# Splitting a projection's weights one stage earlier, and one product for two halves, in a two-block attention kernel

## The chip, the cores and the metric

The kernel runs on one core of one Trainium2 chip, in one launch. The metric is device time in microseconds. The kernel before takes 3167.22 us, the median of 3 runs from 3156.71 to 3170.61.

## The reference

A sequence of 2048 tokens of 1024 channels goes through two blocks, all in fp32.

```python
def first_block(x, ...):
    h = rms_norm(x, g_pre) * (1.0 + scale) + shift
    qa, ka, va, fa, za, qb, kb, vb, zb = split(h @ w_in)
    oa = forgetting_attention(qa, ka, va, fa + b_fgate) * silu(za)      # 8 heads of 64
    qb, kb = rope(qb), rope(kb)                                         # 8 query heads, 2 key heads
    ob = sliding_window_sink_attention(qb, kb, vb, sinks) * silu(zb)    # window of 128
    y = concatenate([oa, ob]) @ w_out
    return x + gate * rms_norm(y, g_post)

def second_block(x, ...):
    h = concatenate([meta_tokens, x])                                   # 16 + 2048 rows
    q_a, c_kv, q_idx, k_idx, w_idx, gate_a, q_h, f_h, i_h, gate_h = split(h @ w_in_2)
    a = dsa_attention(q_a, rms_norm_2(c_kv), q_idx, k_idx, w_idx, rel_bias, w_uk, w_uv) * silu(gate_a)
    r = rms_norm_2(hgrn2(q_h, f_h, i_h)) * silu(gate_h)
    y = concatenate([a, r]) @ w_out_2                                   # 1024 x 1024
    return layer_norm(DN_ALPHA * h + y)[16:]

def rope(x, positions):       # per head: the first 32 channels and the last 32
    x1, x2 = x[..., :half], x[..., half:]
    return concatenate([x1 * cos - x2 * sin, x2 * cos + x1 * sin])
```

`dsa_attention` lets every query see the meta rows and its 256 best keys by an index score; `hgrn2` is a gated recurrence over chunks of 64.

## The kernel before

Values and weights of fp32 are split into a high and a low fp16 part, and a product is three fp16 products (high by high, high by low, low by high) summed in PSUM. A 128-column product over 1024 channels for 512 tokens is so 24 matmuls (`mm3_T`, L319). The Tile scheduler fixes the order of each engine's instructions ahead of time from the program order and its priorities; on the chip every engine and every DMA queue works its list in that order. Nearly all DMAs of the parts below are issued by SyncE.

**The stages**, by the profile: a prologue; the first projection (`blocks1`), woven from about 200 us on with the forgetting attention, to about 950 us; the rest of that attention, the sliding attention and the first output projection, to about 1500; the second projection (`phase_proj2`) with the index scores and the top-k selection, to about 2215; and the third stage (`phase_dsa`), in which 32 steps of the sparse attention (4 groups of queries by 8 heads) are woven with the recurrence's chunks and the second output projection with its norm.

**Weights of a projection** come in blocks through `stream` (L298), which loads one block ahead. `load_w` (L249) loads a block in four pieces of 256 KB into a ring of 4 buffers with tag "wraw" (L260), squares each on ScalarE (L262) and sums the squares over the partitions with a small matmul `wsum` (L239 in `sum_scale`), for which the result bank has the tag "st" and rotates with products of that tag. From the sum come a scale and, per piece, a product by it on VectorE (L282), a cast to the high part `whi` on ScalarE (L283) and the low part `wlo` on GpSimd (L284). The second projection has twelve blocks: forget gate, gates, queries of the attention, queries of the recurrence and the input gate, two each (`fh fh gh gh ga ga qh qh qa qa ih ih`). Each product of a block of queries leaves PSUM by `evac_T` (L361: `ehi` on ScalarE L345, low part on VectorE L346, store L366). VectorE also runs the selection's scans (L1788) in this stage.

**The second output projection's weights** are used in the third stage. After the fourth block `wo_scale` (L1097) loads them once, through the same ring, for their scale alone. `phase_dsa` calls `load_wo` in its first step, with priority −3000, and that loads them again, in 8 pieces of 512 KB, into a single buffer, and splits them:

```python
    for k in range(KK):
        raw = rp.tile([128, D], F32, name="raw", tag="z" if tag == "pp" else "xr", bufs=2 if tag == "pp" else 1)
        nc.sync.dma_start(raw, src[k * 128:(k + 1) * 128])                             # L1116
        for c in (slice(0, 512), slice(512, D)):
            nc.scalar.activation(hi[:, k, c], raw[:, c], AF.Copy, scale=K.ows)         # L1118
            nc.vector.scalar_tensor_tensor(lo[:, k, c], raw[:, c], K.ows, hi[:, k, c], ...)  # L1119
```

**The sliding attention's keys and queries** are rotated as they leave PSUM, in `rotated` (L504). Its weights are laid out with the first halves of the heads' channels ahead of the second halves: 2 key heads give m = 64 columns of each half, the queries m = 128. For each of 4 groups of 512 tokens it makes two products, one for each half, in two banks of tag "pp", and combines them with the tables of cosines and sines: two products by a table on VectorE (L523, L524) and an addition or subtraction on GpSimd (L525), in tiles `ra` of a ring of 4, stored by `store_rot` (L477).

## Time and profile before

| | before |
|---|---|
| median of 3 runs | 3167.22 us |
| the profiled execution | 3170.48 us |
| its span | 3168.7 us |
| its granted TensorE clock, mean | 0.938 |
| TensorE busy | 2822.7 us, 89% |
| VectorE, ScalarE, GpSimd busy | 66%, 53%, 46% |

The profile records one execution. Its span runs from the first to the last instruction, and the execution's own time lies 1.8 us above it. Times in the rows are counted from the start of the span. Matmuls are pipelined: one that is recorded as 0.38 us long may have its successor start 0.22 us after it.

### The profile page before, as it was taken

How to read it: one execution, taken by the hardware profiler on the slowest of the kernel's cores; microseconds unless marked ns; L12 is line 12 of the kernel's file. 1: busy time of each engine (PE TensorE's matmuls, PEld its weight loads, DVE VectorE, ACT ScalarE, POOL GpSimd, SP SyncE). 2: the span in 40 equal slices, each digit the busy share in tenths (PEclk: the TensorE clock that was granted, in tenths of full speed). 3: DMA queues.
4: the chain of work that ended last, by engine and by line, in shares of the span. 5: the costliest groups of instructions: out<-in, count | busy, mean ns of one | idle time of the engine just before them, and what ended most of it. 6: DMA issues, size and time to landing. Idle time of an engine off the chain costs nothing. (4 is left out here: it accounts for less than half of the span.)

```text
span 3168.7 us, 65862 instructions
## 1 busy us (share of the span) xinstructions
PE 2822.7 (89%) x25152; PEld 1858.8 (59%) x25152; DVE 2101.6 (66%) x5073; ACT 1686.9 (53%) x3058; POOL 1450.2 (46%) x1241
## 2 busy tenths in 40 slices
PE   7899999999997899999998889899678888988997
PEld 5554444477884555544445665358566566666663
DVE  7523765566678676646499699830578778888763
ACT  4423665576566655634356466321455456657763
POOL 3211446564333555534233433610456567768752
PEclk9899999999996799999999989899679989999998
DMA  6222343532235343334433532222753444443331
GB/s 235 82 87 84 105 129 111 173 95 69 79 94 167 109 142 108 124 91 157 111 97 101 160 125 73 89 91 63 182 159 102 137 133 113 118 117 110 122 97 59
DMA packets 271184, 364.28 MB, mean 115 GB/s; under 512 B 60205, under 2 KB 192033, under 8 KB 269705
## 3 DMA queue, kind: packets, MB, share of 16 engines
q1 hardware_dynamic: 270424, 359.96, 37.8%
q8 instruction: 199, 3.26, 0.4%
q14 instruction: 129, 1.05, 0.1%
q10 hardware_dynamic: 432, 0.02, 0.0%
HBM read 247.05 MB, written 112.82 MB: 114 GB/s over the span
## 5 line engine op out<-in xcount | busy, mean ns | idle before, releaser
L752 POOL TENSOR_TENSOR plo<-p,phi 128x512 f16<-128x512 f32 (+3 forms) x600 | 664.9, 1121 | 569.9 <-ACT phi L748 360.0
L748 ACT CAST phi<-p 128x512 f16<-128x512 f32 (+3 forms) x649 | 347.0, 554 | 84.2 <-PE po L778 75.1
L746 ACT ACTIVATE p<-pst,shift,dci 128x512 f32<-128x512 f32 (+4 forms) x352 | 247.4, 716 | 137.2 <-POOL plo L752 46.7
L778 PE MATMUL po<-v,plo 128*128 128x65 f16 x2176 | 270.1, 196 | 35.0 <-POOL plo L752 27.9
L776 PE MATMUL po<-v,phi 128*128 128x65 f16 x2176 | 286.4, 197 | 5.3 <-ACT phi L748 4.2
L777 PE MATMUL po<-v,phi 128*128 128x64 f16 x2176 | 285.3, 198 | 0.0
L778 PEld LDWEIGHTS <-plo 128*128 128x128 f16 x2424 | 234.7, 101 | 79.2 <-POOL plo L752 46.8
L746 ACT ACTIVATE p<-pst,shift,fci 128x512 f32<-128x512 f32 (+1 forms) x320 | 220.1, 710 | 113.1 <-PE pst L984 70.2
L963 DVE TENSOR_REDUCE mu<-p 128x1 f32<-128x512 f32 (+2 forms) x320 | 188.4, 603 | 130.1 <-PE p L959 83.3
L776 PEld LDWEIGHTS <-phi 128*128 128x128 f16 x2424 | 236.1, 100 | 48.8 <-ACT phi L748 11.4
L284 POOL TENSOR_TENSOR wlo<-wraw,whi 128x512 f16<-128x512 f32 (+3 forms) x116 | 149.9, 1310 | 216.9 <-ACT whi L283 214.0
L2058 DVE CUSTOM_DVE_ANT_0 jk<-p,mk 128x512 bf16<-128x512 f32 (+2 forms) x320 | 193.4, 604 | 80.5 <-PE p L2052 32.8
L777 PEld LDWEIGHTS <-phi 128*128 128x128 f16 x2424 | 235.6, 100 | 15.3 <-issue 1.8
L337 PE MATMUL pp<-whi,hhi 128*128 128x256 f16 (+2 forms) x824 | 235.0, 286 | 7.7 <-ACT whi L283 5.7
L339 PE MATMUL pp<-whi,hlo 128*128 128x256 f16 (+2 forms) x824 | 233.2, 285 | 4.2 <-POOL hlo L465 4.2
L338 PE MATMUL pp<-wlo,hhi 128*128 128x256 f16 (+2 forms) x824 | 234.7, 285 | 0.6 <-POOL wlo L284 0.6
L326 PE MATMUL pp<-hhi,whi 128*128 128x512 f16 (+2 forms) x496 | 190.7, 384 | 4.4 <-DVE ra L523 4.4
L328 PE MATMUL pp<-hhi,wlo 128*128 128x512 f16 (+2 forms) x496 | 190.3, 384 | 0.0
L327 PE MATMUL pp<-hlo,whi 128*128 128x512 f16 (+2 forms) x496 | 190.0, 383 | 0.0
L328 PEld LDWEIGHTS <-wlo 128*128 128x128 f16 (+2 forms) x1000 | 99.7, 100 | 122.6 <-POOL wlo L284 10.9
L326 PEld LDWEIGHTS <-whi 128*128 128x128 f16 (+2 forms) x1000 | 100.5, 101 | 120.1 <-issue 10.2
L327 PEld LDWEIGHTS <-whi 128*128 128x128 f16 (+2 forms) x1000 | 99.9, 101 | 117.3 <-issue 16.0
(666 smaller groups left out, 8933.6 us busy)
## 6 DMA issues: line engine op xcount, KB each, us to landing
wraw<-in_w_in_dram SPq DMA_DIRECT2D x88, 256.0 KB
d_z<-er SPq DMA_DIRECT2D x128, 128.0 KB
bT<-d_rb SPq DMA_DIRECT2D x32, 384.0 KB
wa<-in_w_ada_dram SPq DMA_DIRECT2D x8, 1024.0 KB
x<-in_x_dram SPq DMA_DIRECT2D x16, 512.0 KB
d_k<-ehi SPq DMA_DIRECT2D x32, 256.0 KB
d_q<-ehi SPq DMA_DIRECT2D x32, 256.0 KB
QA<-d_q SPq DMA_DIRECT2D x64, 128.0 KB
```

What stands on the lines that cost most here:

```text
L326: nc.tensor.matmul(ps, lhsT=whi, rhs=hhi[:, kk, :], start=kk == 0, stop=False)
L327: nc.tensor.matmul(ps, lhsT=whi, rhs=hlo[:, kk, :], start=False, stop=False)
L328: nc.tensor.matmul(ps, lhsT=wlo, rhs=hhi[:, kk, :], start=False, stop=kk == KK - 1)
L337: nc.tensor.matmul(ps, lhsT=hhi[:, kk, s], rhs=whi, start=kk == 0, stop=False)
L338: nc.tensor.matmul(ps, lhsT=hhi[:, kk, s], rhs=wlo, start=False, stop=False)
L339: nc.tensor.matmul(ps, lhsT=hlo[:, kk, s], rhs=whi, start=False, stop=kk == KK - 1)
L746: nc.scalar.activation(p, s, AF.Exp, scale=ci[:m], bias=K.shift[:m])
L748: nc.scalar.copy(hi, p)
L752: e.tensor_tensor(lo, p, hi, op=ALU.subtract)
L776: nc.tensor.matmul(o, lhsT=hi, rhs=v[:, :65], start=first, stop=False, **kw)
L777: nc.tensor.matmul(o[:, 1:65], lhsT=hi, rhs=v[:, 65:129], start=False, stop=False, **kw)
L778: nc.tensor.matmul(o, lhsT=lo, rhs=v[:, :65], start=False, stop=last, **kw)
```

## The change

For the rotated keys (m = 64) one product with all 128 columns takes the place of two with 64. Its first 64 rows are the one operand, and ScalarE copies its last 64 rows to a fifth tile of the `ra` ring, whose first row is partition 0, for the other. The queries are made as before.

The split of the second output projection's weights moves into the second projection. `wo_parts` stands in the list of blocks between the two blocks of queries `qa`: 16 rounds, each loading 256 KB into the "wraw" ring, casting, subtracting and storing both parts to DRAM (`d_wo`) from a tile of the same ring. The third stage reads the parts with four DMAs of 1 MB (`read_wo`), with the priority that `load_wo` had.

```diff
             for g in range(NG):
-                p = [ps.tile([128, 512], F32, name="pp")[:m] for _ in range(2)]
-                for a in range(2):
-                    mm3_T(K, p[a], w, a * m, h[g])
+                if m == 64:
+                    pb = ps.tile([128, 512], F32, name="pp")
+                    mm3_T(K, pb, w, 0, h[g])
+                    z = sp.tile([128, 512], F32, name="ra", tag="ra", bufs=4)[:m]
+                    nc.scalar.copy(z, pb[m:])
+                    p = [pb[:m], z]
+                else:
+                    p = [ps.tile([128, 512], F32, name="pp")[:m] for _ in range(2)]
+                    for a in range(2):
+                        mm3_T(K, p[a], w, a * m, h[g])
...
+def wo_parts(K, pool, src):
+    nc = K.nc
+    for k in range(KK):
+        for c in range(2):
+            raw = pool.tile([128, 2, 256], F32, name="wraw", tag="wraw", bufs=K.rbufs).rearrange("p a n -> p (a n)")
+            nc.sync.dma_start(raw, src[k * 128:(k + 1) * 128, c * 512:c * 512 + 512])
+            x = pool.tile([128, 2, 512], F16, name="wparts", tag="wraw", bufs=K.rbufs)
+            nc.scalar.activation(x[:, 0], raw, AF.Copy, scale=K.ows)
+            nc.vector.scalar_tensor_tensor(x[:, 1], raw, K.ows, x[:, 0], op0=ALU.mult, op1=ALU.subtract)
+            nc.sync.dma_start(K.d_wo[:, :, k, c * 512:c * 512 + 512].rearrange("i p n -> p i n"), x)
+
+def read_wo(K, pool):
+    hi, lo = (pool.tile([128, KK, D], F16, name=n) for n in ("wohi", "wolo"))
+    for i, x in enumerate((hi, lo)):
+        for k in range(0, KK, 4):
+            K.nc.sync.dma_start(x[:, k:k + 4], K.d_wo[i, :, k:k + 4])
+    return hi, lo
...
-        stream(K, wp, pst, [*blocks[:4], lambda: wo_scale(...), *blocks[4:10], lambda: rel_rows(...), *blocks[10:]], "st")
+        stream(K, wp, pst, [*blocks[:4], lambda: wo_scale(...), *blocks[4:9], lambda: wo_parts(K, wp, A["w_out_2"]),
+                            blocks[9], lambda: rel_rows(...), *blocks[10:]], "st")
...
-                    whi, wlo = load_wo(K, wp, A["w_out_2"], os_, "y")
+                    whi, wlo = read_wo(K, wp)
```

The lines of the new code in the changed kernel are L1123 (load), L1125 (cast), L1126 (subtraction) and L1127 (store); lines behind them move down by 30.

**SyncE's queue in the tail of the second projection.** Before, between the loads of the last two blocks (L260) stand stores of query products (L366) and of the selection's masks (L1797):

```order
L260 DMA wraw<-in_w_in_dram 128x512 x2
L1387 DMA d_qh<-e_25700 128x512
L1797 DMA d_mask<-jk 128x1536
L260 DMA wraw<-in_w_in_dram 128x512 x2
L366 DMA d_q_143<-ehi 256x1x512 x4
...
L366 DMA d_q_143<-ehi 256x1x512 x3
L260 DMA wraw<-in_w_in_dram 128x512 x2
L366 DMA d_q_143<-ehi 256x1x512 x2
L260 DMA wraw<-in_w_in_dram 128x512 x2
L366 DMA d_q_143<-ehi 256x1x512 x6
```

and now, where the first of the 16 rounds stand and where the last one ends:

```order
L1828 DMA d_mask<-jk 128x1536
L1123 DMA wraw<-in_w_out_dram 128x512
L366 DMA d_q_144<-ehi 256x1x512 x2
L1127 DMA d_wo<-wparts 128x2x512
L1123 DMA wraw<-in_w_out_dram 128x512
L366 DMA d_q_144<-ehi 256x1x512 x2
L1127 DMA d_wo<-wparts 128x2x512
L1123 DMA wraw<-in_w_out_dram 128x512
...
L1123 DMA wraw<-in_w_out_dram 128x512
L1127 DMA d_wo<-wparts 128x2x512
L260 DMA wraw<-in_w_in_dram 128x512 x2
L1127 DMA d_wo<-wparts 128x2x512
L260 DMA wraw<-in_w_in_dram 128x512 x2
```

What moved: the 16 rounds stand between the loads of the second query block and those of the input gate's block (L260 in the last rows). In the first six rounds a load (L1123) stands behind the store (L1127) of the round before.

**ScalarE in the same place.** Before, the second query block's last two casts (L283) stand behind a square and an eviction, and the next block's squares (L262) between evictions:

```order
L345 ACTIVATE ehi<-st,inv_25762 128x512
L283 CAST whi<-wraw 128x512 x2
L262 ACTIVATE wjk,wam<-wraw 128x512
L345 ACTIVATE ehi<-pp,inv_25762 128x512
L262 ACTIVATE wjk,wam<-wraw 128x512
L345 ACTIVATE ehi<-psc,inv_26055 128x512
L283 CAST whi<-wraw 128x512 x2
L345 ACTIVATE ehi<-st,inv_26055 128x512
L262 ACTIVATE wjk,wam<-wraw 128x512 x2
L345 ACTIVATE ehi<-pp,inv_26055 128x512
```

and now:

```order
L345 ACTIVATE ehi<-st,inv_25671 128x512
L283 CAST whi<-wraw 128x512
L1125 ACTIVATE wparts<-wraw,ows 128x512
L283 CAST whi<-wraw 128x512
L1125 ACTIVATE wparts<-wraw,ows 128x512
L345 ACTIVATE ehi<-pp,inv_25671 128x512
L1125 ACTIVATE wparts<-wraw,ows 128x512 x2
L345 ACTIVATE ehi<-psc,inv_26060 128x512
L1125 ACTIVATE wparts<-wraw,ows 128x512 x7
L262 ACTIVATE wjk,wam<-wraw 128x512 x4
L345 ACTIVATE rhi<-pt_26304 8x512
L283 CAST whi<-wraw 128x512 x2
```

What moved: the last two casts stand one by one among the casts of the rounds (L1125), and the next block's four squares behind all of those.

**TensorE at the sum of squares of the input gate's block** (`wsum`, L239). Before, it stands behind the 4th matmul of the second query block's second product:

```order
L328 LDWEIGHTS wlo
L328 MATMUL pp<-x1hi_11223,wlo 128x512
L326 LDWEIGHTS whi
L326 MATMUL pp<-x1hi_11223,whi 128x512
L239 MATMUL wsum<-wa_26016,ones 128x1
L326 LDWEIGHTS whi
L326 MATMUL st<-x1hi_11221,whi 128x512
L327 LDWEIGHTS whi
```

and now, where `psc` is the last product ahead of it:

```order
L328 LDWEIGHTS wlo
L328 MATMUL psc<-x1hi_11132,wlo 128x512
L1998 MATMUL pt_26304<-oh,rb 8x512
L190 MATMUL pt_28611<-idf,p2a 1x128
L239 MATMUL wsum<-wa_26021,ones 128x1
L326 LDWEIGHTS whi
L326 MATMUL st<-x1hi_11130,whi 128x512
L327 LDWEIGHTS whi
```

What moved: the second query block's products in the banks `pp`, `psc`, `pp` and `psc`, 24 matmuls each, all stand ahead of `wsum`, and only its three products in the bank `st` behind it.

## Rows read from the trace of the kernel before

**Rows 1.** The page, busy time of each engine in the whole span, with the share of the span and the count of instructions.

```profile
PE 2822.7 (89%) x25152; PEld 1858.8 (59%) x25152; DVE 2101.6 (66%) x5073; ACT 1686.9 (53%) x3058; POOL 1450.2 (46%) x1241
```

**Rows 2.** The table of stretches: for each, from:to in us, its length, then the busy time of TensorE, of its weight loads, of VectorE, ScalarE and GpSimd with their counts, the granted TensorE clock (1 is full), the mean share of the 16 DMA engines, and GB/s.

```profile
430.00:650.00 220.00, 205.01 (x1557) 106.87 (x1558) 124.05 (x263) 120.92 (x246) 134.90 (x125) 0.96 0.42 129
650.00:950.00 300.00, 294.91 (x3546) 247.74 (x3545) 200.14 (x596) 194.17 (x366) 126.60 (x125) 0.99 0.28 85
...
2045.00:2215.00 170.00, 167.77 (x1181) 113.80 (x1178) 37.08 (x82) 40.67 (x80) 26.96 (x25) 1.00 0.25 77
2215.00:2430.00 215.00, 151.89 (x1724) 122.91 (x1725) 153.18 (x335) 113.91 (x196) 111.92 (x90) 0.76 0.59 155
2430.00:2900.00 470.00, 411.97 (x4969) 296.33 (x4968) 381.16 (x774) 277.26 (x451) 319.40 (x238) 0.94 0.42 122
```

**Rows 3.** The chain of waits of 2255 to 2335 us: its shares by line, and one of its pieces (start, us, what).

```profile
by line: DMA raw<-in_w_out_dram 31.3%; DVE wolo L1119 10.5%; issue 7.7%; DVE zrow L763 7.5%; DMA zg<-d_z 4.8%; ACT wohi L1118 4.5%; DVE Ts L1923 3.9%; DVE jk L2058 2.9%; DVE Xl L1912 2.8%; DVE zrow L765 2.5%; PE pst L2103 2.4%; PE pst L2113
...
2334.91 3.85 DMA zg<-d_z
```

**Rows 4.** Groups of instructions by shape on TensorE from 400 to 520 us, where the keys' rotated product stands (`128*64` is the shape of the weights): busy us, mean ns of one, and the idle time before them with what ended it.

```profile
L326 PE MATMUL pp<-hhi,whi 128*64 128x512 f16 x64 | 24.5, 383 | 1.1 <-DVE ra L523 1.1
...
L326 PE MATMUL pp<-hhi,whi 128*128 128x512 f16 x35 | 13.7, 392 | 2.9 <-DVE ra L523 2.9
```

**Rows 5.** The timeline of TensorE at 439 us, inside a product of 64 columns: start, us, engine, line, operation.

```profile
439.06 0.38 PE L328 MATMUL pp<-hhi,wlo 128*64 128x512 f16 x1
439.28 0.38 PE L326 MATMUL pp<-hhi,whi 128*64 128x512 f16 x1
439.49 0.38 PE L327 MATMUL pp<-hlo,whi 128*64 128x512 f16 x1
```

**Rows 6.** Waits of TensorE from 430 to 950 us for the rotated values (total us, times, longest).

```profile
PE pp L326 <- DVE ra L523: 4.4, 3, 2.9
```

**Rows 7.** The tile `ra`, its cast: min/median/max in ns.

```profile
L480 ACT CAST ehi<-ra x24: 601/617/622, 447.0 to 652.3; 128x512 f16<-128x512 f32 x16, 64x512 f16<-64x512 f32 x8
```

**Rows 8.** The timeline of SyncE's DMA issues in the tail of the second projection (a line joins neighbours of one form, and its us run from the first to the end of the last).

```profile
2055.18 1.45 SPq L260 DMA_DIRECT2D wraw<-in_w_in_dram  x2
2061.68 5.21 SPq L366 DMA_DIRECT2D d_q<-ehi  x4
...
2092.38 1.45 SPq L260 DMA_DIRECT2D wraw<-in_w_in_dram  x2
```

**Rows 9.** The same of ScalarE.

```profile
2076.71 1.13 ACT L283 CAST whi<-wraw 128x512 f16<-128x512 f32 x2
...
2093.10 0.69 ACT L345 ACTIVATE ehi<-st,inv 128x512 f16<-128x512 f32 x1 [1.72 <-issue]
2095.39 0.63 ACT L262 ACTIVATE wjk<-wraw 128x512 bf16<-128x512 f32 x1 [1.60 <-DMA wraw<-in_w_in_dram]
```

**Rows 10.** The same of VectorE.

```profile
2057.39 3.62 DVE L1788 TENSOR_TENSOR_SCAN y<-jk 128x1664 f16<-128x1664 bf16 x1
...
2076.22 3.46 DVE L1847 TENSOR_TENSOR dc<-dc 128x256 f32<-128x256 f32 x6
...
2093.82 0.75 DVE L346 SCALAR_TENSOR_TENSOR ehi<-st,inv,ehi 128x512 f16<-128x512 f32 x1 [2.36 <-ACT ehi L345]
```

**Rows 11.** The same of GpSimd.

```profile
2053.68 2.59 POOL L284 TENSOR_TENSOR wlo<-wraw,whi 128x512 f16<-128x512 f32 x2 [1.69 <-ACT whi L283]
...
2077.39 2.27 POOL L284 TENSOR_TENSOR wlo<-wraw,whi 128x512 f16<-128x512 f32 x2 [4.90 <-ACT whi L283]
```

**Rows 12.** The same of TensorE; the time in brackets is idle time before the instruction, and what ended it. `psc` at 2079.59 is the first product of the second block of query weights, `pp` at 2084.77 the one after it, L337 the first of the input gate's block.

```profile
2040.10 0.61 PE L328 MATMUL pp<-x1hi,wlo 128*128 128x512 f16 x1 [5.53 <-POOL wlo L284]
2040.50 0.63 PE L326 MATMUL pp<-x1hi,whi 128*128 128x512 f16 x1
...
2043.38 0.38 PE L327 MATMUL pp<-x1lo,whi 128*128 128x512 f16 x1
...
2079.59 0.38 PE L326 MATMUL psc<-x1hi,whi 128*128 128x512 f16 x1
...
2084.77 0.38 PE L326 MATMUL pp<-x1hi,whi 128*128 128x512 f16 x1
...
2087.43 0.38 PE L239 MATMUL wsum<-wa,ones 128*128 128x1 f32 x2 [1.64 <-DVE wa L237]
...
2124.11 0.28 PE L337 MATMUL pp<-whi,mhi 128*16 128x256 f16 x1
```

**Rows 13.** The subtraction of the second output projection's weights, from 2200 to 2400 us: min/median/max in ns.

```profile
L1119 DVE SCALAR_TENSOR_TENSOR wolo<-raw,ows,wohi x16: 737/752/2655, 2264.8 to 2331.1; 128x512 f16<-128x512 f32 x16
```

**Rows 14.** Waits from 2200 to 2420 us (total us, times, longest).

```profile
DVE wolo L1119 <- ACT wohi L1118: 11.8, 6, 3.1
...
ACT wohi L1118 <- DMA raw<-in_w_out_dram: 10.3, 5, 3.1
```

**Rows 15.** The table of stretches again, for two parts of the third stage's opening (columns as in 2; the DMA share is the last but one).

```profile
2220.00:2230.00 10.00, 5.29 (x26) 4.01 (x23) 3.26 (x24) 0.57 (x1) 1.05 (x1) 0.50 0.93 163
2250.00:2335.00 85.00, 60.96 (x729) 51.84 (x729) 64.41 (x128) 50.52 (x92) 44.33 (x38) 0.76 0.61 160
```

More of the change, by code (lines that the diff above doesn't have):

```diff
@@ L1436, in phase_proj2 @@
         blocks = [(*w2_of(A, cols), K.xinv, set2(kind, cols[0][0]), kind in ("ga", "gh")) for kind, cols in BLK2]
-        stream(K, wp, pst, [*blocks[:4], lambda: wo_scale(K, wp, pst, A["w_out_2"], "st"), *blocks[4:10], lambda: rel_rows(K, A, sp, pt, "pt0"), *blocks[10:]], "st")
+        stream(K, wp, pst, [*blocks[:4], lambda: wo_scale(K, wp, pst, A["w_out_2"], "st"), *blocks[4:9], lambda: wo_parts(K, wp, A["w_out_2"]),
+                            blocks[9], lambda: rel_rows(K, A, sp, pt, "pt0"), *blocks[10:]], "st")
         K.quick.run(tk, QUICK[0], 0)
@@ L2238, in build @@
                 ("d_vf", [10, 128, NT, 129], F16),
-                ("d_o", [S, D], F32), ("d_x1", [S, D], F32), ("d_qi", [256, 2, S], F16), ("d_ki", [64, 2, S], F16),
+                ("d_o", [S, D], F32), ("d_x1", [S, D], F32), ("d_qi", [256, 2, S], F16), ("d_ki", [64, 2, S], F16), ("d_wo", [2, 128, KK, D], F16),
                 ("d_q2", [512, 2, S], F16), ("d_k2", [512, 2, NK], F16),
```

## The prediction

> **What bounds the kernel now.** I read the page's line of busy times first: TensorE is busy for 89% of the span, every other engine for 66% or less [rows 1]. That is a mean over unlike stages, so the stage table comes next [rows 2]. The reader is to see three regimes. From 430 to 950 us (end of the first projection, woven with the first attention) TensorE works 499.9 of 520 us: bound by TensorE. From 2045 to 2215 us (tail of the second projection) it works 167.8 of 170 us while VectorE, ScalarE and GpSimd are almost free. From 2215 to 2430 us (opening of the third stage) it works only 151.9 of 215 us at a granted clock of 0.76; no engine is full, so something is waiting. The chain of waits of 2255 to 2335 us says what [rows 3]: loads of the second output projection's raw weights hold 31.3% of those 80 us, their split on VectorE 10.5% and on ScalarE 4.5%: together 37 us.
>
> **The change, part by part.**
>
> *Keys' rotated halves.* Before, each group of 512 tokens takes two products of 24 matmuls with 64 columns of weights; now one product with 128 columns gives both halves. Four products of 24 go away. A 64-column matmul lasts 383 ns, hardly less than the 392 of a 128-column one [rows 4], and its successors start 0.215 us apart [rows 5]: 96 x 0.215 = 20.6 us of TensorE. It lies in the stage that TensorE bounds at 499.9/520 = 0.96, so I count 19. Upper end: 20.6 plus the 4.4 us in which a product waited for VectorE to free its bank [rows 6], since a group now takes one bank and not two: 25. Lower end 0, if TensorE merely waits there for something else. New are four ScalarE copies of 64x512, priced by the 0.62 us cast of this line's tiles [rows 7]: 2.5 us, covered by a ScalarE that works 120.9 of 220 us there [rows 2]; uncovered they would cost their 2.5. A fifth tile now shares the ring of four, so a rotation may wait one GpSimd addition more; TensorE has attention work ready meanwhile, and I count nothing.
>
> Here the Trainium skill speaks against the change (TensorEngine Tiling (Array Packing), The Solution and Performance Considerations): weights of 64 columns or fewer can run as two independent tiles side by side, up to twice as fast. By that the two half products would already have cost no more than one and the saving would be 0 instead of 19. The starts 0.215 us apart say that this program doesn't run them so [rows 5].
>
> *The split moved into the second projection.* The order shows 16 rounds: load 256 KB, ScalarE cast, VectorE subtraction, store. In rounds 1 to 6 the next load stands behind the previous store on the same queue. I price a round from neighbours: a load issued at 2092.38 was there for ScalarE at 2095.39, 3.0 us [rows 8, 9]; the cast is an eviction's 0.69, the subtraction 0.75 [rows 9, 10]; the store's issue about 0.5 (four in 5.21 us with waits [rows 8] bound it at 1.3). That is 5.0 us. The first load can leave when GpSimd frees a slot, where the load of 2055.18 left [rows 8, 11]. Six rounds are 30 us; a 3.62 us scan and a 3.46 us chain of sums, in front of two of the subtractions on VectorE [rows 10], add some 5: 2090. Two things then go wrong for TensorE.
>
> First, the second query block's last two weight pieces were cast at 2076.71 and finished by GpSimd at 2079.7 [rows 9, 11]. Now the second of these casts stands behind round 6's on ScalarE, and that waits for load 6 until 2088.5; GpSimd ends at 2091. That block's first product, begun at 2079.59 and ended at 2084.77 before [rows 12], ends at about 2092: 7 us late.
>
> Second, the next block's weights (input gate) queue behind all 16 rounds. Rounds 7 to 16 have two loads under way: half of 3.0 + 0.69 + 0.75 + 0.5, with 0.35 on top for queueing behind the other's issue (two loads issue in 1.45 us [rows 8]), is some 2.65 each, to 2116.5. Then the loads (3.0), two squares and the reduction: the sum of squares reaches TensorE at about 2123; before it did at 2087.43, having made TensorE wait 1.64 us [rows 12]. In front of it the changed order leaves four products of 24 x 0.216 = 5.2 us, to 2112.8. TensorE idles 10 us, then has three products to do (15.5 us), and the gate block starts at 2139 and not at 2124.11 [rows 12]: 15 late. Restarting after 5.53 us of idle, matmuls lasted 0.61 us for 3 us before they fell to 0.38 [rows 12]; that adds 1.5. **Cost 17.** Both ends: 0 if all rounds ran at 2.65, since the sum of squares then comes at about 2104, before the fourth product ends; 36 if all ran at 5.0 (2055.2 + 80 + 7 + 15.5 = 2158, 34 late, and the restart). I take the sum of the order, nearer the low end. The 16 casts and subtractions themselves lie on engines with 40.7 and 37.1 busy us of 170 [rows 2].
>
> The Trainium skill (DMA: Bandwidth & Descriptors, Anatomy of one DMA) has a transfer cost about 2.0 us fixed plus its bytes over 436 GB/s, by which my estimate for 256 KB would be 2.6 us and a round 4.6; the six lone rounds would shrink by 2.4 us and the cost from 17 to about 14. The rows' 3.0 is used.
>
> *The third stage's opening.* Eight raw loads, 16 casts and 16 subtractions leave it; four loads of 1 MB come, the same 4 MB. VectorE had 16 x 0.752 = 12.0 us of subtractions [rows 13] and stood 11.8 us waiting for their casts, because ScalarE stood 10.3 us waiting for the raw tile, which has a single buffer [rows 14]. Both queues are in order, so the attention's and the recurrent layer's instructions stood behind. Upper end: the 37 us of the chain, cut by the transfers: they keep the DMA engines 0.61 busy over 85 us, and the highest share of the neighbourhood is 0.93 [rows 15], so 85 us can't fall below 55.8: 29. Lower end 5: the next wait is near, since the chain goes on into another load of 3.85 us [rows 3]. VectorE's own work and wait, 23.8, is the middle; I take **20**, as late loads will take some of it. What is late next: keys, queries and bias tables of the following heads, which now queue behind 1 MB transfers. VectorE and TensorE carry the rest of the stage, 381 and 412 of 470 us [rows 2], so a start 20 us earlier should end 20 us earlier.
>
> *Sum.* -19 + 17 - 20 = -22. The profiled execution took 3170.5 (span 3168.7 and 1.8 around it), 3.3 over the median of the runs, 3167.2. 3170.5 - 22 = **3148**. A measurement of this kernel tells about 0.5%, 15.8 us, from no change: faster means under 3151.4, slower over 3183.1.
>
> **Rivals.**
> A. *The opening gives back all that transfers allow.* 29 for 20: 3139. For it: 37 us on the chain. Against: a DMA share of 0.93 would have to hold for 56 us.
> B. *A new wait takes the old one's place.* The heads' loads, behind 1 MB transfers, end the waits that the raw weights ended. Only 5 is left: 3163. For it: the 3.85 us load on the same chain. Against: VectorE drops 12 us of work whatever waits.
> C. *The one product saves nothing*, either since halves already ran together or because TensorE waits elsewhere: 3167. Against: starts 0.215 us apart, and 0.96 busy.
> D. *Slower: the rounds starve TensorE at the tail of the second projection.* If a round takes 6.0 us (stores and loads of 256 KB hindering each other, VectorE late for each), 16 end at 2151, the gate block starts at 2174, 50 late, 51 with the restart. With 14 from the opening: 3170.5 - 19 + 51 - 14 = 3189. It decides from the point where the loss equals the gains of 39, a mean round of 5.2 us. For it: nothing else in this stretch can feed TensorE. Against: ten rounds have two loads under way.
>
> **How the numbers follow.** Forecast 0.52, A 0.17, B 0.14, C 0.05, D 0.12. The forecast's own range is 3138 to 3160 (split loss 10 to 25, opening 14 to 24), six tenths of it under 3151.4: faster 0.32 + 0.17 = 0.49. The rest of it, 0.20, with B and C is same: 0.39. Slower is D: 0.12. The range 3130 to 3176 leaves out D and A's far end.
>
> **What would show it.** Right: 24 matmuls a group with 128 columns in the rotated keys, and the 950 us mark of before reached some 19 us earlier; TensorE idle about 10 us ahead of the sum of squares in the second projection's tail, with the gate block some 15 us later against the first query product; no raw loads after it, and the first eight heads done some 20 us sooner. Wrong: a tail without that idle stretch, a first stage that ends where it did, or bias, key or query loads that end the waits on ScalarE and VectorE in the opening.

## The result and the profile after

The changed kernel takes 3193.22 us, the median of 4 runs from 3185.53 to 3200.97; the kernel before took 3162.06 beside them. The ratio is 1.0095, 95% interval 1.007 to 1.012: slower by about 30 us. The forecast was 3148, faster by 22. The profiled execution has a span of 3191.7 us, 23.0 over the profile of before, at a mean clock of 0.928.

The page's busy times [rows 1] hardly changed; TensorE has 96 matmuls less:

```profile
PE 2816.5 (88%) x25056; PEld 1852.2 (58%) x25056; DVE 2125.3 (67%) x5073; ACT 1692.8 (53%) x3062; POOL 1440.7 (45%) x1241
```

The stages of the changed kernel (columns as in [rows 2]; the tail and the opening are parted 40 us later, as the second projection ends later):

```profile
430.00:650.00 220.00, 186.93 (x1434) 99.60 (x1433) 131.06 (x263) 118.66 (x241) 138.60 (x127) 0.91 0.44 130
...
2045.00:2255.00 210.00, 184.43 (x1226) 122.11 (x1225) 51.91 (x129) 56.95 (x104) 26.67 (x25) 0.90 0.42 125
2255.00:2430.00 175.00, 136.52 (x1696) 112.83 (x1696) 134.31 (x286) 101.06 (x176) 108.02 (x88) 0.81 0.60 163
```

From 430 to 650 us TensorE works 186.9 us and not 205.0, so the product was saved, and it stands idle for 33 us, not 15, at a granted clock of 0.91, not 0.96 [rows 2]. The tail of the second projection (2045 to 2255 here) has 25.6 us of idle time, before 2.2 in a stretch 40 us shorter, and the opening behind it runs at a clock of 0.81, not 0.76.

TensorE in the tail of the second projection (answers to [rows 12]; L337 is the first product of the input gate's block):

```profile
2082.35 0.39 PE L326 MATMUL psc<-x1hi,whi 128*128 128x512 f16 x1 [2.32 <-ACT whi L283]
...
2086.78 0.61 PE L326 MATMUL psc<-x1hi,whi 128*128 128x512 f16 x1 [1.31 <-ACT whi L283]
...
2121.12 0.59 PE L239 MATMUL wsum<-wa,ones 128*128 128x1 f32 x2 [7.61 <-DVE wa L237]
...
2140.55 0.28 PE L337 MATMUL pp<-whi,mhi 128*16 128x256 f16 x1
```

and SyncE's queue there ([rows 8]; L1123 is a round's load, L260 the next block's):

```profile
2052.29 0.33 SPq L1123 DMA_DIRECT2D wraw<-in_w_out_dram  x1
...
2060.30 0.46 SPq L1123 DMA_DIRECT2D wraw<-in_w_out_dram  x1
...
2066.43 0.46 SPq L1123 DMA_DIRECT2D wraw<-in_w_out_dram  x1
...
2082.49 0.41 SPq L1123 DMA_DIRECT2D wraw<-in_w_out_dram  x1
...
2083.57 0.56 SPq L1123 DMA_DIRECT2D wraw<-in_w_out_dram  x1
...
2108.06 0.46 SPq L1123 DMA_DIRECT2D wraw<-in_w_out_dram  x1
...
2111.33 2.06 SPq L260 DMA_DIRECT2D wraw<-in_w_in_dram  x2
```

ScalarE's casts in the first and the third round, with what they waited for:

```profile
2054.92 0.72 ACT L1125 ACTIVATE wparts<-wraw,ows 128x512 f16<-128x512 f32 x1 [0.56 <-DMA wraw<-in_w_out_dram]
...
2069.81 0.72 ACT L1125 ACTIVATE wparts<-wraw,ows 128x512 f16<-128x512 f32 x1 [5.86 <-DMA wraw<-in_w_out_dram]
```

The second query block's pieces come late twice, by 2.32 and 1.31 us, the sum of squares comes at 2121.12 and not at 2087.43 and is waited for 7.61 us, and the gate block starts at 2140.55, not at 2124.11. The rounds hold the queue from 2052.29 to 2111.33.

The third stage, by the reciprocal with which VectorE ends each of the 32 heads: the 1st, 16th and 32nd, of before

```profile
2245.88 0.17 DVE L785 RECIPROCAL r<-pc 128x4 f32<-128x4 f32 x1
...
2578.62 0.18 DVE L785 RECIPROCAL r<-pc 128x4 f32<-128x4 f32 x1 [0.34 <-ACT pc L2123]
...
3117.69 0.18 DVE L785 RECIPROCAL r<-pc 128x4 f32<-128x4 f32 x1 [0.21 <-ACT pc L2123]
```

and after:

```profile
2261.74 0.18 DVE L793 RECIPROCAL r<-pc 128x4 f32<-128x4 f32 x1
...
2558.30 0.13 DVE L793 RECIPROCAL r<-pc 128x4 f32<-128x4 f32 x1
...
3141.17 0.18 DVE L793 RECIPROCAL r<-pc 128x4 f32<-128x4 f32 x1 [1.21 <-ACT pc L2154]
```

The first head is 15.9 us late, the 16th 20.3 early, the last 23.5 late. In the first half the stage wins 36 us, in the second it gives back 44. Not all of the 36 is the opening's: the experiments below have a kernel with the old weights' path that wins most of it. The waits of [rows 14] are gone with their instructions.

**Where the 23 us are.** Each profile is cut at two marks that all kernels here share: the sum of squares of the first weight block that the stream loads (211.52 us before, 209.13 after) and that of the last gate block (2128.37 and 2144.84). Between them lie 1916.8 us before and 1935.7 after, +18.9; from the last mark to the end 1040.3 and 1046.9, +6.6; ahead of the first -2.4. The forecast had -2 and -20 for the two parts.

### The profile page after: what moved, and what is told of

It reads as the page before. It is cut to its first block, busy times and chain, and to the rows that moved or that the text cites. A ratio compares the mean times of both kernels' runs of the same rounds, so it can differ in the third digit from the quotient of the medians.

```text
span 3191.7 us, 65771 instructions
## 1 busy us (share of the span) xinstructions
PE 2816.5 (88%) x25056; PEld 1852.2 (58%) x25056; DVE 2125.3 (67%) x5073; ACT 1692.8 (53%) x3062; POOL 1440.7 (45%) x1241
## 5 line engine op out<-in xcount | busy, mean ns | idle before, releaser
L760 POOL TENSOR_TENSOR plo<-p,phi 128x512 f16<-128x512 f32 (+3 forms) x600 | 653.8, 1103 | 564.7 <-ACT phi L756 371.1
L785 PEld LDWEIGHTS <-phi 128*128 128x128 f16 x2424 | 235.3, 100 | 18.9 <-issue 3.7
L337 PE MATMUL pp<-whi,hhi 128*128 128x256 f16 (+2 forms) x824 | 234.3, 285 | 10.0 <-ACT whi L283 5.7
L326 PE MATMUL pp<-hhi,whi 128*128 128x512 f16 (+1 forms) x464 | 178.9, 385 | 1.7 <-DVE ra L531 1.2
L327 PE MATMUL pp<-hlo,whi 128*128 128x512 f16 (+1 forms) x464 | 178.4, 385 | 0.0
L328 PE MATMUL pp<-hhi,wlo 128*128 128x512 f16 (+1 forms) x464 | 178.4, 385 | 0.0
L326 PEld LDWEIGHTS <-whi 128*128 128x128 f16 (+1 forms) x968 | 97.3, 101 | 123.1 <-ACT whi L283 15.8
L328 PEld LDWEIGHTS <-wlo 128*128 128x128 f16 (+1 forms) x968 | 96.6, 100 | 124.3 <-POOL wlo L284 13.0
L327 PEld LDWEIGHTS <-whi 128*128 128x128 f16 (+1 forms) x968 | 96.7, 100 | 110.8 <-issue 13.9
```

Of the source, the lines that this page charges most:

```text
L326: nc.tensor.matmul(ps, lhsT=whi, rhs=hhi[:, kk, :], start=kk == 0, stop=False)
L327: nc.tensor.matmul(ps, lhsT=whi, rhs=hlo[:, kk, :], start=False, stop=False)
L328: nc.tensor.matmul(ps, lhsT=wlo, rhs=hhi[:, kk, :], start=False, stop=kk == KK - 1)
L337: nc.tensor.matmul(ps, lhsT=hhi[:, kk, s], rhs=whi, start=kk == 0, stop=False)
L760: e.tensor_tensor(lo, p, hi, op=ALU.subtract)
L785: nc.tensor.matmul(o[:, 1:65], lhsT=hi, rhs=v[:, 65:129], start=False, stop=False, **kw)
```

## Experiments

All ratios are to the kernel before, run on the same chip, with 95% intervals. "To gate" and "gate to end" are the two parts just defined, from the one profiled execution of each. Executions scatter: those of the kernel before on one chip have a standard deviation of 4 to 6 us. So do the parts: two buffers has the lists of before up to the gate (TensorE's and SyncE's row for row) and differs by 7.7 us there, eight reads has those of the changed kernel and differs by 10.2. A single difference under some 10 us is therefore not an effect.

| kernel | ratio | to gate | gate to end |
|---|---|---|---|
| before | 1 | 1916.8 | 1040.3 |
| changed | 1.0095 (1.007 to 1.012) | 1935.7 | 1046.9 |
| keys only | 1.0020 (1.0006 to 1.0035) | 1916.7 | 1047.3 |
| keys from PSUM | 1.0007 (0.9992 to 1.0023) | 1915.4 | 1038.3 |
| keys twice | 1.0141 (1.0123 to 1.0158) | 1952.6 | 1049.5 |
| keys half | 1.0051 (1.0033 to 1.0070) | 1911.8 | 1056.2 |
| queries less | 1.0056 (1.0037 to 1.0075) | 1895.8 | 1067.7 |
| split unused | 1.0069 (1.0047 to 1.0092) | 1931.8 | 1043.0 |
| weights only | 1.0014 (0.9998 to 1.0029) | 1939.8 | 1021.8 |
| PSUM and weights | 1.0026 (1.0008 to 1.0045) | 1936.4 | 1021.8 |
| own ring | 1.0009 (0.9998 to 1.0020) | 1938.9 | 1019.0 |
| own ring, stores by ScalarE | 1.0014 (0.9998 to 1.0030) | 1938.0 | 1022.3 |
| eight reads | 1.0069 (1.0052 to 1.0087) | 1925.5 | 1045.7 |
| stores by ScalarE | 1.0067 (1.0045 to 1.0089) | 1942.1 | 1042.9 |
| PSUM, late split | 1.0008 (0.9995 to 1.0021) | 1918.2 | 1042.3 |
| own ring, late split | 1.0005 (0.9995 to 1.0014) | 1923.1 | 1043.7 |
| early split | 1.0036 (1.0021 to 1.0052) | 1944.1 | 1031.8 |
| two buffers | 1.0041 (1.0024 to 1.0058) | 1909.1 | 1049.2 |
| two buffers, own ring | 0.9995 (0.9979 to 1.0012) | 1912.0 | 1037.2 |
| two buffers, PSUM | 0.9993 (0.9980 to 1.0006) | 1922.3 | 1032.1 |

### The keys' product

*Keys only*: the new `if m == 64` branch in the kernel before. 

> The kernel before with the keys' one product alone (the second projection and the weights of the third stage untouched). Its planned order in the third stage is the changed kernel's: the recurrence's chunks 1 to 6 stand behind 7, 11, 16, 18, 21 and 24 heads and not behind 6, 10, 14, 17, 20 and 23. Theory 'queue': the 20 us that the projection gains are lost again by 950 us, since VectorE holds the attention's row bounds behind rotations; 950 us mark within 3 us of before. Theory 'order': the third stage is 15 to 25 us longer by its order alone, with the old weights' path; total +15 to +25. Rival 'read': the third stage's loss comes from reading the parts from DRAM, so here it is as before and the total is 0 +- 5. Rival 'as predicted': the first stage ends 19 us sooner, total -19.

```profile
430.00:650.00 220.00, 186.82 (x1436) 100.15 (x1435) 132.91 (x261) 117.91 (x240) 137.99 (x125) 0.91 0.43 130
```

The two marks lie 1916.7 us apart, before 1916.8: the product gains nothing. The four kernels here with the one product and no moved split (keys only, keys from PSUM, and those two with two buffers) take 1912.0 to 1922.3 us to the gate, the two with two products (before, two buffers) 1916.8 and 1909.1; a gain of 19 would stand out of that. TensorE's 18 us less of work (columns as in [rows 2]) are 18 us more of idle time. The theory 'queue', that a held VectorE loses them, starts from this place in the changed kernel, VectorE first:

```profile
460.29 5.07 DVE L531 SCALAR_TENSOR_TENSOR ra<-ra,inv,cs 64x512 f32<-64x512 f32 x1 [2.32 <-POOL ehi L481]
465.28 1.12 DVE L773 SCALAR_TENSOR_TENSOR zrow<-zrow,t 128x4 f16<-128x4 f16 x1
```

GpSimd:

```profile
460.22 3.37 POOL L284 TENSOR_TENSOR wlo<-wraw,whi 128x512 f16<-128x512 f32 x3
463.55 1.26 POOL L533 TENSOR_TENSOR ra<-ra 64x512 f32<-64x512 f32 x1
464.77 1.59 POOL L284 TENSOR_TENSOR wlo<-wraw,whi 128x512 f16<-128x512 f32 x1
```

and TensorE:

```profile
466.45 0.64 PE L776 MATMUL p<-idh,zrow 128*66 128x128 f16 x4 [7.92 <-DVE zrow L773]
```

A rotation that reads the copied half waits 2.32 us for GpSimd, then lasts 5.07 us where its like takes 0.73, until four GpSimd instructions in a row (460.22 to 464.8) are over; the attention's row bound `zrow` queues behind it, and TensorE waits 7.92 us. The next run takes that away.

*Keys from PSUM*: no copy, no fifth tile; VectorE reads partitions 64 to 127.

```diff
-                    nc.scalar.copy(z, pb[m:])
-                    p = [pb[:m], z]
+                    p = [pb[:m], pb[m:]]
...
+                iv = [inv[:m], inv[m:]] if m == 64 else [inv, inv]
...
-                    nc.vector.scalar_tensor_tensor(x, p[a], inv[:m], tb[0], ...)
+                    nc.vector.scalar_tensor_tensor(x, p[a], iv[a], tb[0][a], ...)
```

> The keys' one product alone, without the copy: VectorE reads the second half from PSUM on partitions 64 to 127 and writes to partitions 0 to 63, so that no rotation reads two operands from SBUF and the ring holds four tiles as before. Theory 'queue' in its form 'GpSimd holds VectorE' or 'fifth tile': the 950 us mark 10 to 19 us sooner than before. Rival 'attention': TensorE's saved time is not on the path of the attention's steps; the mark is within 5 us of before. Theory 'order' (chunks behind 6, 10, 15, 18, 21 and 24 heads): the third stage 5 to 20 longer; rival 'read': as before.

```profile
430.00:650.00 220.00, 186.74 (x1410) 98.64 (x1411) 126.25 (x258) 115.09 (x236) 133.66 (x123) 0.91 0.44 129
```

The held rotation is gone (all 48 rotations last 0.73 to 0.76 us), and TensorE's idle time is the same 33 us, spread over other waits. So the wait of 7.92 us is real but not the cause; 'queue' falls, as far as it means a held rotation.

What took the saving's place can be counted. The weight block whose sum of squares stood 413.9 us behind the first mark before stands at 397.6 with keys only and at 398.3 with keys from PSUM: the projection is 16 us ahead there. Two blocks on, 523.3 us behind the mark before, it stands at 525.4 and 535.0: nothing is left. Meanwhile the attention has fallen behind. TensorE's matmuls on its score tile `pst` (time, count, then clock and DMA), of before and with keys only:

```profile
430.00:650.00 220.00, 35.46 (x154) 0.96 0.42 129
```

```profile
430.00:650.00 220.00, 34.25 (x142) 0.91 0.43 130
```

On the attention's tiles `p`, `po` and `pst` together they are 934 before, 867 with keys only and 852 with keys from PSUM. With keys only TensorE's longest waits in this stretch are for the attention's steps on VectorE and ScalarE (8.2, 5.7, 3.6 and 3.5 us). I read this as the projection moving ahead of an attention that did not get faster and had to be finished all the same; no run shows it by itself.

*Keys twice*: every one of the keys' products is made twice, 192 matmuls more. 

> The kernel before with each of the keys' eight products of 24 matmuls made twice: 192 matmuls of 64 columns more, 192 x 0.215 = 41 us of TensorE. If TensorE bounds that stage, as the prediction had it: the 950 us mark 38 to 41 later, total +35 or more. Theory 'cover' (the attention's chain of short steps sets the pace and the projection fills its gaps): 15 us of idle time are left there to fill, so the mark is at most 26 later; with the clock held up by the work, less. The third stage's order differs from before's: 0 to 20 more either way in the total.

```profile
430.00:650.00 220.00, 206.94 (x1527) 104.41 (x1524) 109.14 (x223) 101.15 (x192) 111.78 (x103) 0.97 0.34 100
```

The first part grows by 35.8 of 41 us, and the idle time is not filled (13 us here, 15 before). So 'cover' falls too: more work costs nearly its full price in the same place where less work gains nothing.

*Keys half* and *queries less*: 96 matmuls less in other ways. Keys half makes the old two products over half of the channels, queries less makes the first of each two products of the rotated queries so; both leave the rest of those sums out.

> The kernel before with each of the keys' eight products made over half of the channels, 12 matmuls and not 24 (the other half of the sum is left out): 96 matmuls fewer, as in the change, but two banks, two products and no copy as before. Theory 'stretch': the saved 20.6 us become idle time of TensorE between 430 and 650 us (30 us or more, before 15), the 950 us mark within 5 of before. Rival 'form' (the one product, its copy or its single bank lose it): idle time 15 to 20, the mark 14 to 20 sooner.

> The kernel before with the first of each two products of the rotated queries made over half of the channels (8 products of 12 matmuls and not 24; the rest of their sums is left out): 96 matmuls of 128 columns fewer, 20.6 us. Theory 'stretch': the 950 us mark within 6 of before. Rival 'TensorE bounds the stage': 14 to 20 sooner.

```profile
430.00:650.00 220.00, 192.51 (x1505) 103.13 (x1501) 134.18 (x274) 120.82 (x245) 142.81 (x132) 0.95 0.44 133
```

Keys half, without any new form, gains 5.0 up to the gate, no more than the scatter; queries less gains 21.0, its full price, though its idle time is 27 us here. So it is not the form of the new product, and the stretch can pay for 96 matmuls elsewhere. In queries less the attention did not fall behind: 921 matmuls on its three tiles, 907 in keys half. What a saving is worth seems to depend on where the planned lists put the attention's work around it. Which row of the lists does that was not found.

### The split in the tail

*Split unused*: `wo_parts` added, `load_wo` kept. 

> The kernel before with the split added in the second projection and its stored parts not used: the third stage still loads and splits the weights itself. Its planned order there has the chunks 1 to 6 behind 6, 9, 15, 17, 21 and 24 heads. The tail of the second projection alone: +17 to +20. Theory 'order': a further 5 to 20 in the third stage, total +22 to +40. Rival 'read': the third stage as before, total +17 to +20.

The first part grows by 15.0, with weights only by 23.0, in the changed kernel by 18.9, with eight reads by 8.7: forecast 17. The tail alone tells it better. From the sum of squares of the second query block to the last gate mark the twelve kernels with no rounds there (late and early split among them) take 80.7 to 83.3 us, and split unused, weights only, PSUM and weights, own ring (with and without stores by ScalarE), eight reads and the changed kernel 99.7 to 102.3, against 82.7 before 17.0 to 19.6 more. The ratio of split unused, 1.0069, is 22 us in all.

*Stores by ScalarE*, in the changed kernel:

```diff
-            nc.sync.dma_start(K.d_wo[:, :, k, c * 512:c * 512 + 512]..., x)
+            nc.scalar.dma_start(K.d_wo[:, :, k, c * 512:c * 512 + 512]..., x)
```

> The changed kernel with the 16 stores of the parts issued by ScalarE and not by SyncE: no load stands behind a store. VectorE's planned list of the third stage is row for row the changed kernel's. Theory 'queue in the tail': rounds of 2.6 to 3 us throughout, 42 to 48 us in all (59 before), the gate block 10 to 15 sooner, total 3178 to 3186, still slower than before by the third stage's order. Rival 'bytes' (256 KB each way need 3.6 us a round): no change, 3190 to 3200.

ScalarE's casts, with what they waited for, and TensorE's sum of squares:

```profile
2075.32 0.72 ACT L1125 ACTIVATE wparts<-wraw,ows 128x512 f16<-128x512 f32 x1 [5.61 <-DMA d_wo<-wparts]
...
2081.14 0.72 ACT L1125 ACTIVATE wparts<-wraw,ows 128x512 f16<-128x512 f32 x1 [4.52 <-DMA d_wo<-wparts]
```

```profile
2129.26 0.59 PE L239 MATMUL wsum<-wa,ones 128*128 128x1 f32 x2 [11.22 <-DVE wa L237]
```

No load stands behind a store any more, and the first rounds still take 5.8 us (2075.32 to 2081.14): the next cast waits for a store, since its tile is a slot of the ring that the store must leave. The wait for the sum of squares is 11.22, not less, and the tail is 22.0 us longer than before. So the order on the queue is not what makes the rounds serial. I read these rows as the ring of four, which the rounds share with the waiting pieces of the query block; a ring of their own was not tried.

*Late split*: `wo_parts` behind `blocks[10]`, with keys from PSUM or the own ring.

> The keys' second half read from PSUM, and the split moved behind the first input gate block, where nothing but that stage's stores queues behind its rounds. The tail of the second projection: gate block within 4 us of before, where the changed kernel had +17. With the opening's 16 to 20 us won: 3145 to 3155 if its planned order (chunks behind 6, 10, 15, 18, 21, 24 heads) is no worse than that of the weights alone; 3165 to 3180 if the order costs 20. Rival: the rounds hold ScalarE's evictions of the gate products, and the tail costs 15 again: 3165 to 3175.

> The changed kernel with the fifth tile in a ring of its own and the split moved behind the first input gate block. VectorE's planned list of the third stage is 98% that of the kernel with the own ring alone, whose third stage took 904 us from the first head done to the end. Theory 'order' and the tail's cost of 17 to 20 by queueing: gate block within 4 us of before, third stage 900 to 912, total 3148 to 3158. Rival 'late split harms the opening' (its casts and stores lie nearer to it; the other kernel with the late split had 919): 3163 to 3172.

SyncE's queue in the kernel with the own ring (L379 is the first head's load):

```profile
2139.18 0.35 SPq L1123 DMA_DIRECT2D wraw<-in_w_out_dram  x1
...
2144.14 0.44 SPq L1123 DMA_DIRECT2D wraw<-in_w_out_dram  x1
...
2182.12 0.42 SPq L1123 DMA_DIRECT2D wraw<-in_w_out_dram  x1
...
2204.72 0.44 SPq L1123 DMA_DIRECT2D wraw<-in_w_out_dram  x1
...
2219.40 0.57 SPq L379 DMA_DIRECT2D QA<-d_q  x1
```

The first part is now only 1.4 and 6.3 us longer, but the first nine rounds start 5.0 to 5.8 us apart among the gate block's stores, the last at 2204.72, and the first head's load leaves 84.5 us after the last gate mark (2134.88), before 73.7 (2202.11 after 2128.37). The tail's cost moved behind the mark. *Early split* (behind `blocks[5]`) 

> The changed kernel, keys as there, with the split between the second block of gates of the recurrence's half and the first of the attention's (right behind its scale), not between the query blocks. VectorE's planned list of the third stage is 98% that of the kernel with the own ring, though the first stage is the changed kernel's. Theory 'order': third stage 900 to 912 from the first head done to the end (930 in the changed kernel). The split's own cost there by queueing: the next block's weights late, 5 to 20. Total 3155 to 3175. Rival 'keys as in the changed kernel cost 20 in any order': 3180 to 3195.

 The first part grew by 27.3: dearer there. The ratio of 1.0036 is 11 us; from the 3167 of before, 'order' had forecast at most 8 more and its rival at least 13. Its third stage is taken up below.

### The third stage

*Weights only*: the changed kernel with the keys' two products. 

> The changed kernel with the keys' two products as before: the moved split and the read from DRAM alone. All theories: the input gate's block starts 15 to 20 us later. Theory 'order' and rival 'read' both: the heads are 20 to 36 us ahead of themselves halfway through the third stage and lose it again, total +15 to +25. Rival 'as predicted': -3 (17 lost, 20 won).

Its 1st, 16th and 32nd head:

```profile
2263.67 0.17 DVE L785 RECIPROCAL r<-pc 128x4 f32<-128x4 f32 x1
...
2559.84 0.17 DVE L785 RECIPROCAL r<-pc 128x4 f32<-128x4 f32 x1
...
3121.36 0.18 DVE L785 RECIPROCAL r<-pc 128x4 f32<-128x4 f32 x1 [0.21 <-ACT pc L2146]
```

From the gate to the end 1021.8 us, 18.5 under before, near the forecast's 20. But the kernels differ in the order of the stage as well, so one pair doesn't price the opening. From the last gate mark to the 16th head, all seven kernels with the old weights' path (two buffers left aside) take 420.9 to 450.2 us and all eight with the moved one (the late split left aside) 402.9 to 415.2: on average 22 less, so the opening's gain is there. Before is the longest of the first group; keys only takes 420.9, so 29 of the 37 us between before (450.2) and the changed kernel (413.3) come without the moved split. To the end the first group takes 1038.3 to 1067.7, the second 1019.0 to 1046.9: on average 17 less, but the two overlap.

The total of weights only is 1.0014, so neither part alone explains the changed kernel: 6 us for the keys and 4 for the weights against 30 for both. What differs is the order that the planner wrote for the third stage. The recurrence's eight chunks stand in VectorE's planned list, its instructions in the order fixed ahead of time, behind so many heads:

| kernel | heads ahead of each chunk |
|---|---|
| before | 1, 6, 10, 14, 17, 20, 23, 25 |
| changed, eight reads, stores by ScalarE (one list, row for row) | 1, 7, 11, 16, 18, 21, 24, 25 |
| weights only, PSUM and weights (one list, row for row) | 1, 7, 10, 16, 18, 21, 24, 25 |
| own ring, with and without stores by ScalarE (one list) | 1, 6, 10, 15, 18, 21, 24, 25 |

*PSUM and weights*: 

> The changed kernel with the keys' second half read by VectorE from PSUM (no copy, no fifth tile). VectorE's planned list in the third stage is, row for row, that of the weights alone with two key products (third stage 935 us, chunks behind 7, 10, 16, 18, 21, 24 heads), not that of the changed kernel (960 us; 7, 11, 16, 18, 21, 24). Theory 'order': third stage 930 to 940, total within 6 us of the weights alone (3166 to 3178). Rival 'interplay' (keys and weights together lose 20 for a reason other than the order): 3187 to 3198 as the changed kernel. If the two parts only added: 3168 + 4 + 2 = 3174, the same as 'order' gives.

*Own ring*: the copied half in a ring of its own, `name="rz", tag="rz", bufs=2`. 

> The changed kernel with the fifth tile in a ring of its own (two buffers), all else the same; VectorE still reads two SBUF operands for two of the four products. Its planned order in the third stage is another one (chunks behind 6, 10, 15, 18, 21, 24 heads). Theory 'order': the third stage takes 930 to 950, not the changed kernel's 960; total 3165 to 3185. Rival 'interplay': 3187 to 3198. On the first stage: theory 'fifth tile' has the 950 us mark 5 or more us sooner than in the changed kernel; rival 'GpSimd holds VectorE' leaves it.

*Eight reads*: `read_wo` in pieces of 512 KB. 

> The changed kernel with the parts read by eight transfers of 512 KB in place of four of 1 MB. VectorE's planned list in the third stage is row for row the changed kernel's. Theory 'order': within 6 us of the changed kernel (3187 to 3200). Rival 'read' (the late keys, queries and tables stand behind 1 MB transfers): 3170 to 3185.

*Own ring, stores by ScalarE*: 

> The same with the fifth tile in its own ring, whose planned list of the third stage took 904 us from the first head on. Theories 'queue in the tail' and 'order' together: 10 to 15 under the kernel with the own ring alone (which was 3 over before), so 7 to 12 faster than before, 3156 to 3162 where before has 3168. Rival 'bytes': as the own ring alone.

Kernels with one list take nearly one time from the gate on: 1046.9, 1045.7 and 1042.9; 1021.8 and 1021.8; 1019.0 and 1022.3. The work in the third stage is the same in all seven, but for the size of the reads in one. The engines' busy times from the gate to the end say so (columns as in [rows 2]), of the changed kernel and with weights only:

```profile
2144.84:3191.70 1046.86, 893.15 (x10194) 653.38 (x10192) 699.95 (x1454) 558.06 (x929) 581.45 (x461) 0.91 0.40 115
```

```profile
2149.36:3171.20 1021.84, 884.75 (x10192) 649.22 (x10192) 699.75 (x1454) 555.58 (x929) 581.91 (x461) 0.92 0.41 118
```

What differs is mostly idle time of TensorE: 152 to 154 us in the three kernels of the first list, 130 to 137 in the four of the other two. A further pair, keys twice and keys half, has one list too (TensorE's and SyncE's agree row for row) and takes 1049.5 and 1056.2. The ratios say it without the marks: 1.0067 to 1.0095 for the first list, 1.0009 to 1.0026 for the other two. Size and count of the reads don't matter. The same wait even returns at the same instruction, a score product of 256 columns, in the changed kernel, with eight reads and with stores by ScalarE:

```profile
2721.40 0.37 PE L2083 MATMUL p<-KA,QA 66*128 66x256 f16 x1 [6.51 <-DVE mu L2089]
```

```profile
2711.89 0.37 PE L2083 MATMUL p<-KA,QA 66*128 66x256 f16 x1 [6.49 <-DVE mu L2089]
```

```profile
2725.16 0.37 PE L2083 MATMUL p<-KA,QA 66*128 66x256 f16 x1 [5.34 <-DVE mu L2089]
```

The two kernels with the own ring wait 5.6 and 5.9 us at such a product too, so this wait marks a list and is not the 25 us.

The heads ahead of the chunks tell lists apart; they are not the list and don't give its time. Keys only has the counts of the changed kernel, but 815 of its 1792 VectorE rows behind the last gate mark differ, and keys from PSUM has the counts of the own ring and takes 1038.3. 'Order', as it was put for these counts, missed twice with the old weights' path: from the gate on keys only is 7.0 longer than before (15 to 25 expected), split unused 2.7 (5 to 20). Early split has the keys of the changed kernel and nearly the list of the own ring (61 of 1794 VectorE rows differ); its 1031.8 lies between the two. So the form of the keys alone doesn't set the third stage's time.

*Two buffers*: the kernel before, the raw weights of the third stage in two buffers by turns.

```diff
-... tag="z" if tag == "pp" else "xr", bufs=2 if tag == "pp" else 1)
+... tag="z" if tag == "pp" else ("xr", "a2")[k % 2], bufs=2 if tag == "pp" else 1)
```

> The kernel before with the raw weights of the third stage loaded into two buffers by turns. No change ahead of the third stage. Theory 'single buffer': the 10 us of ScalarE's wait and most of VectorE's 12 go; third stage 10 to 18 shorter, 3150 to 3158, plus or minus the spread of the order (28 us over kernels of the same work so far). Rival 'VectorE's work': VectorE still does 16 subtractions; 0 to 5 shorter, plus or minus the same.

> The same, with the keys' one product and the copied half in a ring of its own. Theory 'single buffer' with nothing from the keys: as the run with two buffers alone, within the spread of the order; 3140 to 3175.

> The same, with the keys' one product read from PSUM. As above: 3140 to 3175.

The waits of [rows 14], 11.8 and 10.3 us, fell with two buffers to

```profile
ACT wohi L1118 <- DMA raw<-in_w_out_dram: 6.6, 4, 2.4
...
DVE wolo L1119 <- ACT wohi L1118: 2.9, 2, 1.9
```

and the time did not: 1.0041, 0.9995 and 0.9993. 'Single buffer' is not confirmed; whatever it is worth lies within what a new order does. No kernel here is measurably faster than before.

## Why the prediction was wrong

- **What bounds the kernel.** The three regimes were read rightly, but 0.96 busy was taken as a rate of exchange. In that stretch 41 us more cost 35.8; 20.6 less gained 21.0 in the queries and, within the scatter, nothing in the keys (0.1 and 5.0).
- **Keys, -19.** Failed: 0 (keys only). The step that failed is "the stage that TensorE bounds at 499.9/520 = 0.96, so I count 19". The saved time is idle time of TensorE, 33 us and not 15, and the attention, which it waits for, is 67 of 934 matmuls behind. The range's lower end, 0 "if TensorE merely waits there for something else", named the condition. The rule on tiles of 64 columns played no part: 18 us of TensorE work did go away.
- **Split, +17.** Right: 15.0 to 23.0, in the changed kernel 18.9. The steps held as well: sum of squares at 2121.12 (forecast 2123), idle 7.61 (10), gate block at 2140.55 (2139). The five rounds up to 2082.49 took 6.0 us each, where 5.0 and two delays (35 us for six) were forecast, later ones 2.7 ((2108.06 - 2083.57)/9). A load that stood behind a round's store took up to 3.4 us from issue to its cast (2066.43 to 2069.81 on ScalarE), more than the row's 3.0. The first round's load, with no store of a round ahead of it, took 2.6 (2052.29 to 2054.92). The Trainium skill's fixed part and rate (DMA: Bandwidth & Descriptors, Anatomy of one DMA), which that section gives for transfers issued by GpSimd, make 2.6 by estimate: the first load agrees, the loads of the following rounds do not.
- **Opening, -20.** Right in size on average (22 less to the 16th head, 17 less to the end, with lists that differ; 18 to 21 less than before in the four kernels with the two other lists), and not there at the end of the changed kernel: +6.6. The step that failed is "a start 20 us earlier should end 20 us earlier", which takes the rest of the stage as fixed. The scheduler, which plans the engines' lists, had written another order for it, and that order is 21 to 28 us longer than others of the same work.
- **The sum.** 0 + 18.9 + 6.6 - 2.4 is the 23 us of the profile. All of the error is in two terms, 19 and 27 us. By the medians the change is 31 us, since the profiled execution of before, from which the forecast counted, lies 8 us over the median beside the result.
- **The rivals.** D was on the right side with the right number, 3189, by luck, since its mechanism did not happen: a mean round took 3.7 us ((2111.33 - 2052.29)/16) and not 6.0. C named the keys' nothing, with a chance of 0.05. None named the re-planned third stage. That it was re-planned could be seen ahead of the run: the planned lists of both kernels have the chunks in other places, in a stage that the change barely touches, and I compared them only around the edits. Whether the new order was faster or slower could not be read from that.

Open: what in a planned list makes it 25 us longer, and which rows of the first stage's list let the attention fall behind. The waits are spread over many places, and no run took a single one of them away with the list kept. That the list sets the time rests on the agreement of kernels that share one.

## What to carry to other kernels

Where a planner orders the engines' lists, an edit is also a new draw of every list behind it: compare the planned lists in the stages that were not edited, and widen the range by what orders of the same work differ by (here 25 to 30 us of 1040). Judge a part by runs that share a list with the kernel they are compared with. A busy share near 1 in a woven stage prices more work, but less work only where the other stream keeps up.

## What the runs showed of the hardware

VectorE's instructions with both operands in SBUF can last much longer while GpSimd is busy. In the changed kernel eight rotations read both operands from SBUF: the two without GpSimd beside them last 0.73 and 0.74 us, those with GpSimd busy all the while 0.86 to 5.07. Where one operand lies in PSUM, GpSimd makes no difference: all 48 rotations of keys from PSUM last 0.73 to 0.76, 23 of them with GpSimd busy throughout. A decay product of the recurrence (128x128) takes 0.28 us undisturbed. The first fence has one of the changed kernel, the second the same instruction in the kernel with PSUM and weights, also with GpSimd busy, and the third GpSimd beside the first:

```profile
2712.69 4.86 DVE L1878 TENSOR_TENSOR dc<-dc 128x128 f32<-128x128 f32 x1
```

```profile
2706.08 1.24 DVE L1878 TENSOR_TENSOR dc<-dc 128x128 f32<-128x128 f32 x1
```

```profile
2710.60 1.62 POOL L760 TENSOR_TENSOR wmlo<-p,wmhi 16x512 f16<-16x512 f32 x1
2712.19 1.59 POOL L760 TENSOR_TENSOR plo<-p,phi 128x512 f16<-128x512 f32 x1
2713.75 1.26 POOL L2179 TENSOR_TENSOR a<-a,z 128x512 f32<-128x512 f32 x1
2714.97 2.42 POOL L1943 TENSOR_TENSOR Xl<-kq,Xh 128x1024 f16<-128x1024 f32 x1
```

4.86 and 1.24 us for 0.28; beside the first GpSimd is busy without a gap from 2710.6 to 2717.4. This is not peculiar to the changed kernel: the kernel before has one of 4.85. The Trainium skill says (SBUF — State Buffer, SBUF: two separate sides) that such a VectorE instruction and a GpSimd instruction that reads SBUF shut each other out, the later one for the whole instruction of the first. The trace agrees, and the rotation shows that VectorE can lose to several GpSimd instructions in a row. That rule spoke against the copy of the change and was not weighed; its price here was not the cause, as keys from PSUM shows.
